# Pre-norms by one product with the mean on all partitions, a and b on four column groups, decode outputs transposed four heads at once

## The chip, the core and the metric

The kernel runs on one core of a Trainium2 chip. The metric is the device time of one execution in microseconds. The core has five engines that run side by side, each through its own instruction list in order: TensorE (PE in the profile; its weight loads are shown as PEld), VectorE (DVE), ScalarE (ACT), GpSimd (POOL) and SyncE (SP, which here only issues DMAs). They meet through semaphores. Activations and weights are in SBUF, matmul results in PSUM, which this kernel uses as eight banks of 128 partitions x 512 float32 values.

## The reference, cut to what matters

One layer of a hybrid decoder on 256 prompt tokens and 8 x 4 decode tokens, 288 columns in all, in float32. Every sub-layer has a norm before it and one behind it:

```python
def rmsnorm(x, g):
    y = x * lax.rsqrt(jnp.mean(x * x, axis=-1, keepdims=True) + EPS)
    return y * g

x = x + 0.5 * rmsnorm(swiglu(rmsnorm(x, f1_pre), f1_wg, f1_wu, f1_wd), f1_post)
proj = rmsnorm(x, mix_pre) @ w_in          # B, C, hc, q, k, v, z, a, b
...
g = -jnp.exp(a_log) * softplus(a + dt_bias)
beta = sigmoid(b)
o, s_new = gated_delta_chunked(l2norm(q) * 128**-0.5, l2norm(k), v, g, beta, s0)
o = rmsnorm(o, dn_norm) * silu(z)          # per head, transposed back in the kernel
out = concat([y_a, o], axis=-1) @ w_out
x = x + rmsnorm(out, mix_post)
x = x + 0.5 * rmsnorm(swiglu(rmsnorm(x, f2_pre), f2_wg, f2_wu, f2_wd), f2_post)
gate = sigmoid(rmsnorm(x, ple_pre) @ w_ple_gate)
x = x + rmsnorm(gate * (p @ w_ple_proj), ple_post)
```

The model width D is 2048, the FFN width 5632; a and b are 8 columns each of the mixer's input projection, one per head.

## The kernel before

**Layout.** Activations are kept transposed: features on the 128 partitions, the 288 tokens as columns. X holds 16 k-tiles of 128 x 288. The weights pass once from HBM as chunks of 128 x 512, four weight tiles of 128 x 128, on SP's DMA queue into six raw buffers. ACT casts a chunk to a rounded form `hi` (L133), DVE makes the remainder `lo` = raw - hi (L134); there are four buffers for such pairs. The activations are split in the same way into XH and XL. Each weight tile then costs three products of 288 columns: hi by XH (L361), hi by XL (L362) and lo by XH (L364). PE therefore spends nearly all its time on triples of these.

**Banks.** Five PSUM banks, "acc", form a ring for outputs that add up; three, "small", take everything else, and also the outputs beyond the fifth when more are open at a time.

**A matmul stage** (`gemm_steps`) starts with a group of outputs that advance together by k, since X itself is still being finished by the stage before: seven outputs in the FFNs and the gate, six in the mixer, five in the output projection. After that come outputs one by one. `prep(k)` finishes the k-tile k of X (adds the residual, squares it into the running sum `sq`, splits it) and is called four chunks ahead of the products that need it.

**The pre-norm** does not touch X. The products use unnormalised X with the gain folded in, and the norm's factor, one value per token, is multiplied into each output when it leaves PSUM: by L445 (`gu_t`) in the FFNs, L560 and L563 (`cvin`) in the mixer, L1132 (`gt`) in the gate. So it is needed when the first output of the first group is finished. `Later.after` makes it in three steps, one per chunk, once all k-tiles are through:

1. `join`: the two halves of the running sum are added (DVE).
2. `columns`: three products (L285) with a column of ones bring the sums of 128 tokens each onto the partitions, 128 x 3; the root (ACT), then on DVE v, a reciprocal, and a Newton step on 128 x 3 (L291, L229 to L232).
3. `kept`, with `rows`: three products (L300, L304) with the identity spread the factors over all partitions, and DVE copies the 128 x 288 result from PSUM (L310).

The mixer's value is `mix.value`, the gate's `ple.value`.

**a and b.** Their weights, 16 k-tiles of 128 x 16, lie in WS, split into 16 columns hi and 16 columns lo. `ab_side` (L587) runs behind each triple of the first output of the mixer's first group: two products, with XH and with XL, into a bank `ab` of 32 partitions, 32 products in all (L592). Their norm is L594, the gates' transposes are in `gates` (L631).

**Decode outputs.** Behind the delta rule, each head's output is transposed back (L960, L961 for the two prompt halves, L963 for the 32 decode tokens of that head, on 32 x 32) and multiplied with gain and z on DVE.

**Order.** The kernel is recorded in program order, and a scheduler sets the order of each engine's instructions when the program is built. An edit at one place can therefore move instructions of other places. In the mixer, `delta` is a generator that issues the gates and the delta rule step by step between the chunks of the input projection.

The functions that the change touches:

Of the kernel before, what the change touches and what calls it, by code (L numbers as in the profile page):

```python
# [41 lines left out]
GATE_START = 16  # L42
ROW_WAIT = 6
LAG = 1
SOLVE_STEPS = 2
# [100 lines left out]
def tile_hymba_step(ctx: ExitStack, tc: tile.TileContext, a: dict):  # L146
# [87 lines left out]
    epst = pers.tile([P, 1], F32, name="epst")  # L234
    nc.gpsimd.memset(epst, EPS)

    def sqrt_table(after):
# [6 lines left out]
    nc.gpsimd.memset(HOT, 0.0)  # L244
    nc.gpsimd.memset(HOT[:, 2:3], 1.0)

    class SquareSum:
# [29 lines left out]
        def columns(self, name, n_warm=0):  # L277
# [15 lines left out]
            rsqrt(self.cols, v, 3, s)  # L293

        def rows(self, name):

            pr = small(f"row_{name}")
            cols = self.cols
            for g in range(2):
                nc.tensor.matmul(  # L300
                    pr[:, g * P : (g + 1) * P], cols[:, g : g + 1].to_broadcast([P, P]), ID, start=True, stop=True
                )
# [24 lines left out]

    def gemm_steps(order, kt, rhs, done, prep=None, extra=None, rate=0, side=None, every=1, fill=(), fine=False):


# [3 lines left out]
        for c in range(len(order) // CH):  # L334
# [19 lines left out]
            for i in range(CH):  # L354
# [9 lines left out]
                nc.tensor.matmul(o, lo[:, i, :], xh, start=False, stop=seen[m] == kt)  # L364
                if side and m == order[0][0]:
                    side(k)
                if seen[m] == kt:
# [6 lines left out]
    def x_parts(k):  # L374
        return XH[:, k, :], XL[:, k, :]
# [38 lines left out]
    class Later:  # L414
# [91 lines left out]

    WS = tmp.tile([P, KD, 32], F32R, tag="qksq", bufs=1, name="WS")

    emb = []

    def loads():
# [19 lines left out]
        for _ in range(4):  # L531
            yield
        split(WS[:, :, 0:16], WS[:, :, 16:32], WR)

# [49 lines left out]

    finished, ab = [], []

    def ab_side(k):  # L587

        if k == 0:
            ab.append(small("ab")[:32, :N])  # L590
        for i, x in enumerate(x_parts(k)):
            nc.tensor.matmul(ab[0], WS[:, k, :], x, start=k == i == 0, stop=k == KD - 1 and i == 1)  # L592
# [38 lines left out]
    def gates():  # L631

        pab = small("pab")
        abd = dl.tile([P, 4, DT], F32, tag="junk", bufs=2, name="abd")
        nc.vector.tensor_copy(abd[:32], ABT[:32, None, SEQ:N].to_broadcast([32, 4, DT]))
        for g in range(3):
            src = ABT[:32, g * P : (g + 1) * P] if g < 2 else abd[:32].rearrange("p a b -> p (a b)")
            nc.tensor.matmul(pab[:, 16 * g : 16 * g + 16], src, C[:32, C_ID2 : C_ID2 + 16], start=True, stop=True)
        AB = tmp.tile([P, 3, 16], F32, tag="AB", bufs=1, name="AB")
# [267 lines left out]
    def delta():  # L907
        while 56 not in finished:
            yield
        for _ in range(GATE_START):  # L910
            yield
# [42 lines left out]
        YB = big.tile([P, H, N], F32, tag="LQ", name="YB")  # L954
        last.append(YB)
        for h in range(H):
            while 48 + h not in finished:
                yield
            po = small("oT")
            nc.tensor.transpose(po[:, 0:P], OB[:, h, :], ID)  # L960
            nc.tensor.transpose(po[:, P : 2 * P], OB[:, 8 + h, :], ID)  # L961
            r = slice(32 * (h % 4), 32 * (h % 4) + 32)
            nc.tensor.transpose(po[:, SEQ:N], OB[r, 16 + h // 4, :], ID[r, r])  # L963
            for c, z in ((slice(0, SEQ), V[:, h, :]), (slice(SEQ, N), VD[:, h, :])):
                nc.vector.scalar_tensor_tensor(
                    YB[:, h, c], po[:, c], C[:, C_DNN : C_DNN + 1], z, op0=ALU.mult, op1=ALU.mult
                )
            yield
# [46 lines left out]

    gemm(ORD["qkv"], KD, x_parts, qkv_done, mix, work, 1, ab_side, fill=fill_mix())
    mrow = mix.value
# [234 lines left out]
```

## Time and profile before

| | |
|---|---|
| Median of 3 runs | 2382.6 us (2380.88 to 2384.11) |
| Profiled execution, its own time | 2383.07 us |
| Span of that execution | 2381.3 us |
| Granted TensorE clock, mean | 0.997 |
| PE busy | 2357.7 us, 99% |
| DVE busy | 1473.1 us, 62% |
| ACT busy | 1165.9 us, 49% |
| POOL busy | 147.4 us, 6% |
| Read from HBM | 386.68 MB, 166 GB/s over the span |

How to read the profile's rows. A group row has the line, engine, operation, output <- input, the shape, and behind "x" the count; then the busy time in us and the mean of one in ns; then the idle time of the engine just ahead of these instructions, and what ended it. A timeline row begins with the start in us from the span's start and the time to the end of the row's last record; "x3" says that three records of one kind stand in it. A matmul's record is longer than the step from one to the next, since matmuls are pipelined: the pace is read from starts. A row of the list of waits has the waiting engine and tile, the releaser, and us in all, count and longest. A row of a windows table has the stretch and its length, then busy time and count of PE, PEld, DVE, ACT and POOL, the granted clock, the DMA share and the rate in GB/s. Numbers of a timeline come from the one profiled execution.

### The profile page before, as it was taken

How to read it: one execution, taken by the hardware profiler on the slowest of the kernel's cores; microseconds unless marked ns; L12 is line 12 of the kernel's file. 1: busy time of each engine (PE TensorE's matmuls, PEld its weight loads, DVE VectorE, ACT ScalarE, POOL GpSimd, SP SyncE). 2: the span in 40 equal slices, each digit the busy share in tenths (PEclk: the TensorE clock that was granted, in tenths of full speed). 3: DMA queues.
4: the chain of work that ended last, by engine and by line, in shares of the span. 5: the costliest groups of instructions: out<-in, count | busy, mean ns of one | idle time of the engine just before them, and what ended most of it. 6: DMA issues, size and time to landing. Idle time of an engine off the chain costs nothing.

```text
span 2381.3 us, 47494 instructions
## 1 busy us (share of the span) xinstructions
PE 2357.7 (99%) x17904; PEld 2336.5 (98%) x17904; DVE 1473.1 (62%) x2788; ACT 1165.9 (49%) x2222; POOL 147.4 (6%) x283
## 2 busy tenths in 40 slices
PE   9999999999999999999999999999999999999997
PEld 9999999999999999999999999999999999999997
DVE  6554555555555688888556577655555555555695
ACT  6444443444444567544455455544443444444474
POOL 0000000000000003122110002430000000000001
PEclk9999999999999999999999999999999999999999
DMA  7665665566656555565444566775656666666654
GB/s 233 172 165 166 167 166 167 165 168 165 167 166 167 166 161 147 162 188 162 129 140 129 167 174 175 226 216 165 168 165 166 167 167 165 166 167 166 187 156 124
DMA packets 213238, 399.07 MB, mean 168 GB/s; under 512 B 24183, under 2 KB 25616, under 8 KB 213008
## 3 DMA queue, kind: packets, MB, share of 16 engines
q1 hardware_dynamic: 207792, 377.73, 56.3%
q0 software_dynamic: 5072, 18.24, 2.5%
q8 instruction: 140, 2.29, 0.4%
q14 instruction: 90, 0.74, 0.1%
q10 hardware_dynamic: 144, 0.07, 0.0%
HBM read 386.68 MB, written 9.26 MB: 166 GB/s over the span
## 4 chain that ended last, share of the span: by engine, by line
PE 60%; DVE 1%; issue 0%; DMA 0%; ACT 0%; POOL 0%; DVEq 0%; ACTq 0%
PE acc L361 19%; PE acc L364 19%; PE acc L362 19%; DVE lo L134 0%; PE pkq L714 0%; DVE Y L1145 0%; PE po L882 0%; PE p L797 0%; DMA S<-in_state_delta 0%; PE pu L993 0%; PE pn L877 0%; DVE cvout L572 0%; PE p L787 0%; PE pd L893 0%; PE pS L870 0%
## 5 line engine op out<-in xcount | busy, mean ns | idle before, releaser
L134 DVE TENSOR_TENSOR lo<-raw,hi 128x512 fp32r<-128x512 f32 (+1 forms) x1417 | 990.5, 700 | 759.6 <-ACT hi L133 736.8
L133 ACT CAST hi<-raw 128x512 fp32r<-128x512 f32 (+1 forms) x1417 | 876.7, 620 | 1124.2 <-PE acc L362 1009.3
L361 PE MATMUL acc<-XH,hi 128*128 128x288 f32 x4096 | 1217.1, 298 | 2.2 <-ACT hi L133 1.2
L364 PE MATMUL acc<-XH,lo 128*128 128x288 f32 x4096 | 1213.1, 297 | 2.2 <-DVE lo L134 2.0
L362 PE MATMUL acc<-XL,hi 128*128 128x288 f32 x4096 | 1197.0, 292 | 0.0
L362 PEld LDWEIGHTS acc<-XL,hi 128*128 128x128 f32 x4096 | 780.4, 191 | 0.3 <-issue 0.2
L361 PEld LDWEIGHTS acc<-XH,hi 128*128 128x128 f32 x4096 | 770.4, 188 | 9.5 <-ACT hi L133 3.9
L364 PEld LDWEIGHTS acc<-XH,lo 128*128 128x128 f32 x4096 | 768.3, 188 | 3.7 <-DVE lo L134 3.3
L362 PE MATMUL acc<-hl_f,hi 128*128 128x288 f32 x1408 | 415.5, 295 | 0.0
L364 PE MATMUL acc<-hh_f,lo 128*128 128x288 f32 x1408 | 415.3, 295 | 0.0
L361 PE MATMUL acc<-hh_f,hi 128*128 128x288 f32 x1408 | 414.5, 294 | 0.0
L364 PEld LDWEIGHTS acc<-hh_f,lo 128*128 128x128 f32 x1408 | 264.8, 188 | 0.0
L362 PEld LDWEIGHTS acc<-hl_f,hi 128*128 128x128 f32 x1408 | 264.3, 188 | 0.0
L361 PEld LDWEIGHTS acc<-hh_f,hi 128*128 128x128 f32 x1408 | 264.0, 187 | 0.0
L445 DVE TENSOR_TENSOR gu_t<-acc,rows_ffn_f 128x288 f32<-128x288 f32 x176 | 79.9, 457 | 51.9 <-PE acc L364 51.6
L465 DVE TENSOR_TENSOR Y<-Y,acc 128x288 f32<-128x288 f32 x96 | 43.5, 453 | 28.1 <-PE acc L364 28.1
L558 POOL MEMSET cvin<- 128x3 f32 (+1 forms) x32 | 3.3, 102 | 900.9 <-PE acc L364 854.4
L1109 POOL DMA_DIRECT2D PJ<-pj_dram x3 | 1.6, 531 | 665.9 <-PE acc L364 665.9
L451 DVE TENSOR_TENSOR gu_t<-gu_t 128x288 f32<-128x288 f32 x88 | 41.3, 471 | 1.8 <-ACT gu_t L447 1.8
L319 ACT ACTIVATE XH<-X,G 128x288 fp32r<-128x288 f32 x64 | 34.3, 536 | 13.2 <-DVE X L398 12.9
L317 DVE TENSOR_TENSOR hl_f<-gu_t,hh_f 128x288 fp32r<-128x288 f32 x88 | 39.6, 452 | 0.0
L572 DVE SCALAR_TENSOR_TENSOR cvout<-cvin,CW,cvout 128x312 f32<-128x312 f32 x72 | 37.4, 536 | 2.9 <-ACT cvout L570 2.3
(369 smaller groups left out, 1239.3 us busy)
## 6 DMA issues: line engine op xcount, KB each, us to landing
raw<-in_gu SPq DMA_DIRECT2D x703, 256.0 KB, 2.7
raw<-in_dn SPq DMA_DIRECT2D x352, 256.0 KB, 2.7
raw<-in_qkv SPq DMA_DIRECT2D x96, 256.0 KB, 2.7
raw<-in_conv SPq DMA_DIRECT2D x96, 256.0 KB, 2.7
raw<-in_out SPq DMA_DIRECT2D x64, 256.0 KB, 2.7
raw<-in_gate SPq DMA_DIRECT2D x64, 256.0 KB, 2.7
raw<-in_z SPq DMA_DIRECT2D x32, 256.0 KB, 2.6
S<-in_state_delta POOLq DMA_DIRECT2D x8, 512.0 KB, 5.5
```

Source lines behind the costliest of these rows:

```text
L133: self.hi = nc.scalar.copy(hi[:, r], t[:, r]).ins
L134: nc.vector.tensor_tensor(lo[:, r], t[:, r], hi[:, r].bitcast(F32), op=ALU.subtract)
L317: nc.vector.tensor_tensor(lo, src, hi.bitcast(F32), op=ALU.subtract)
L319: first = nc.scalar.activation(hi, src, AF.Copy, scale=gain).ins
L361: nc.tensor.matmul(o, hi[:, i, :], xh, start=seen[m] == 0, stop=False)
L362: nc.tensor.matmul(o, hi[:, i, :], xl, start=False, stop=False)
L364: nc.tensor.matmul(o, lo[:, i, :], xh, start=False, stop=seen[m] == kt)
L445: nc.vector.tensor_tensor(t, ps, prep.value, op=ALU.mult)
L451: nc.vector.tensor_tensor(t, t, s, op=ALU.mult)
L465: nc.vector.tensor_tensor(Y[:, m, :], Y[:, m, :], ps, op=ALU.add)
L558: nc.gpsimd.memset(e[:, 0:w], 0.0)
L572: nc.vector.scalar_tensor_tensor(c[:, 0:n], e[:, j : j + n], wcols[:, j : j + 1], c[:, 0:n], op0=ALU.mult, op1=ALU.add)
```

## The change

**Pre-norms.** `SquareSum.direct` takes the place of `columns` and `kept` for the four pre-norms (both FFNs, mixer, gate); the norms behind the sub-layers stay as they were. One float32 product has the constant 0.25/D as its weights in all 128 x 128 places and the running squares as its 288 columns: every partition of the bank receives a quarter of the mean, for all tokens. ACT takes the root of it plus EPS/4 (s). DVE then makes r = 1/s, w = (ms + EPS/4) r + s, and 1/w on 128 x 288, which is the factor with one Newton step in it. `Later.after` has two steps in place of three.

**a and b.** WS holds the float32 weights, gain folded in, padded with zeros from 16 to 32 columns. `ab_products` issues 16 products with unsplit X together, on four groups of 32 PE columns by k modulo 4, so the bank holds four partial sums on 128 partitions. `delta` calls it AB_WAIT = 2 steps after the mixer's norm value has been made. The norm's multiplication (ABT) is on 128 partitions, and the gates' transposes add the four partial sums by contracting over 128 partitions.

**Decode outputs.** The 32 x 32 transpose per head goes; at every fourth head one 128 x 128 transpose brings the decode tokens of four heads, and one DVE operation multiplies them.

```diff
@@ SquareSum
+        def direct(self, name):
+            ps = small(f"ms_{name}")[:, :N]
+            for i, x in enumerate(self.parts):
+                nc.tensor.matmul(ps, MEAN.to_broadcast([P, P]), x, start=i == 0, stop=i == len(self.parts) - 1)
+            s = tmp.tile([P, N], F32, tag="rows", name=f"rs_{name}")
+            nc.scalar.activation(s, ps, AF.Sqrt, bias=epsq)
+            r, w = (tmp.tile([P, N], F32, tag=t, name=n) for t, n in (("e0", "rs_w"), ("e1", "rs_u")))
+            nc.vector.reciprocal(r, s)
+            nc.vector.scalar_tensor_tensor(w, ps, EPS / 4, r, op0=ALU.add, op1=ALU.mult)
+            nc.vector.tensor_tensor(w, w, s, op=ALU.add)
+            nc.vector.reciprocal(s, w)
+            return s
-        def kept(self, name):
-            pr = self.rows(name)
-            rows = tmp.tile([P, N], F32, tag="rows", name=f"rows_{name}")
-            nc.vector.tensor_copy(rows, pr)
-            return rows
@@ Later.after
             elif self.stage == 2:
-                self.sq.columns(self.name)
-            elif self.stage == 3:
-                self.value = self.sq.kept(self.name)
+                self.value = self.sq.direct(self.name)
@@ weights of a and b
-    WS = tmp.tile([P, KD, 32], F32R, tag="qksq", bufs=1, name="WS")
+    WS = tmp.tile([P, KD, 32], F32, tag="qksq", bufs=1, name="WS")
...
-        split(WS[:, :, 0:16], WS[:, :, 16:32], WR)
+        nc.vector.memset(WS[:, :, 16:32], 0.0)
+        gain = G[:, GAINS.index("mix_pre"), :, None].to_broadcast([P, KD, 16])
+        nc.vector.tensor_tensor(WS[:, :, 0:16], WR, gain, op=ALU.mult)
@@ mixer
-    def ab_side(k):
-        if k == 0:
-            ab.append(small("ab")[:32, :N])
-        for i, x in enumerate(x_parts(k)):
-            nc.tensor.matmul(ab[0], WS[:, k, :], x, start=k == i == 0, stop=k == KD - 1 and i == 1)
-        if k == KD - 1:
-            nc.vector.tensor_tensor(ABT[:32], ab[0], mix.value[:32], op=ALU.mult)
-            finished.append(56)
+    def ab_products():
+        ab = small("ab")[:, :N]
+        for k in range(KD):
+            r = slice(32 * (k % 4), 32 * (k % 4) + 32)
+            nc.tensor.matmul(
+                ab[r], WS[:, k, :], X[:, k, :], start=k < 4, stop=k >= KD - 4, tile_position=(0, 32 * (k % 4))
+            )
+        nc.vector.tensor_tensor(ABT, ab, mix.value, op=ALU.mult)
+        finished.append(56)
...
     def delta():
-        while 56 not in finished:
+        while mix.value is None:
+            yield
+        for _ in range(AB_WAIT):
             yield
+        ab_products()
@@ transposes of the outputs
-            nc.tensor.transpose(po[:, 0:P], OB[:, h, :], ID)
-            nc.tensor.transpose(po[:, P : 2 * P], OB[:, 8 + h, :], ID)
-            r = slice(32 * (h % 4), 32 * (h % 4) + 32)
-            nc.tensor.transpose(po[:, SEQ:N], OB[r, 16 + h // 4, :], ID[r, r])
...
+            for n in range(2):
+                nc.tensor.transpose(po[:, n * P : (n + 1) * P], OB[:, 8 * n + h, :], ID)
+            if h % 4 == 3:
+                nc.tensor.transpose(po[:, SEQ : SEQ + P], OB[:, 16 + h // 4, :], ID)
+                hs = slice(h - 3, h + 1)
+                gated(YB[:, hs, SEQ:N], po[:, SEQ : SEQ + P].rearrange("p (h t) -> p h t", h=4), VD[:, hs, :])
+            gated(YB[:, h, 0:SEQ], po[:, 0:SEQ], V[:, h, :])
```

What the scheduler makes of it, at three places. The numbers behind tile names count buffers, and the lines of the changed kernel are shifted: L134 is L135 there, L361, L362 and L364 are L374, L375 and L377, L560 and L563 are L572 and L575, L1132 is L1151.

DVE at the gate's pre-norm, before: the 128 x 3 operations, the copy, and the first outputs of the group (`gt`).

```order
L134 TENSOR_TENSOR lo_29064<-raw_28930,hi_29063 128x512
L291 TENSOR_SCALAR rs_v<-ss_ple 128x3
L229 RECIPROCAL rs_r<-rs_s 128x3
L230 SCALAR_TENSOR_TENSOR rs_t<-rs_r 128x3
L231 TENSOR_TENSOR rs_t<-rs_t,rs_v 128x3
L232 SCALAR_TENSOR_TENSOR rc_ple<-rs_t,rs_r 128x3
L134 TENSOR_TENSOR lo_29088<-raw_28948,hi_29087 128x512
L310 COPY rows_ple<-row_ple 128x288
L1132 TENSOR_TENSOR gt<-acc_28510,rows_ple 128x288
```

The same place in the changed kernel:

```order
L135 TENSOR_TENSOR lo_29002<-raw_28873,hi_29001 128x512
L309 RECIPROCAL rs_w<-rs_ple 128x288
L135 TENSOR_TENSOR lo_29020<-raw_28891,hi_29019 128x512
L310 SCALAR_TENSOR_TENSOR rs_u<-ms_ple,rs_w 128x288
L311 TENSOR_TENSOR rs_u<-rs_u,rs_ple 128x288
L135 TENSOR_TENSOR lo_29060<-raw_28914,hi_29059 128x512
L312 RECIPROCAL rs_ple<-rs_u 128x288
L135 TENSOR_TENSOR lo_29110<-raw_28932,hi_29109 128x512
L1151 TENSOR_TENSOR gt<-acc_28453,rs_ple 128x288
```

Where five narrow operations and the copy stood with one split between them, four wide operations now stand with two splits between them and a third ahead of the first `gt`.

PE at the mixer's norm, before: the three column sums stand between two triples, and two products for a and b behind each triple of the first output.

```order
L364 MATMUL acc_10549<-XH,lo_10917 128x288
L285 MATMUL ss_mix<-HOT,sq_pre_f_10433 128x3 x3
L361 MATMUL acc_10512<-XH,hi_10939 128x288
L362 MATMUL acc_10512<-XL,hi_10939 128x288
L364 MATMUL acc_10512<-XH,lo_10940 128x288
L592 MATMUL ab<-XH,WS 32x288
L592 MATMUL ab<-XL,WS 32x288
L361 MATMUL acc_10519<-XH,hi_10939 128x288
```

The same in the changed kernel:

```order
L374 MATMUL acc_10535<-XH,hi_10952 128x288
L304 MATMUL ms_mix<-sq_pre_f_10426,MEAN 128x288
L604 MATMUL ab<-X,WS 32x288 x16
L375 MATMUL acc_10535<-XL,hi_10952 128x288
L377 MATMUL acc_10535<-XH,lo_10953 128x288
L374 MATMUL acc_10539<-XH,hi_10952 128x288
L375 MATMUL acc_10539<-XL,hi_10952 128x288
L377 MATMUL acc_10539<-XH,lo_10953 128x288
L374 MATMUL acc_11142<-XH,hi_10980 128x288
```

The norm's product and all 16 products for a and b now stand together inside the triples of the last k-tile of the six-output group; `acc_11142`, five weight products behind, is the seventh output, the first one behind the group.

DVE at the mixer's norm in the changed kernel:

```order
L309 RECIPROCAL rs_w<-rs_mix 128x288
L310 SCALAR_TENSOR_TENSOR rs_u<-ms_mix,rs_w 128x288
L311 TENSOR_TENSOR rs_u<-rs_u,rs_mix 128x288
L135 TENSOR_TENSOR lo_11137<-raw_10911,hi_11136 128x512
L312 RECIPROCAL rs_mix<-rs_u 128x288
L572 TENSOR_TENSOR cvin<-acc_10505,rs_mix 128x256
L575 TENSOR_TENSOR cvin<-acc_10505,rs_mix 128x8x4
```

One split stands between the wide operations here, ahead of the second reciprocal; the first output of the group is read by the two `cvin` rows behind it.

More of the change, by code (lines that the diff above doesn't have):

```diff
@@ L43 @@
 ROW_WAIT = 6
+AB_WAIT = 2
 LAG = 1
@@ L235, in tile_hymba_step @@
     nc.gpsimd.memset(epst, EPS)
+    epsq = pers.tile([P, 1], F32, name="epsq")
+    nc.gpsimd.memset(epsq, EPS / 4)
     def sqrt_table(after):
@@ L245, in tile_hymba_step @@
     nc.gpsimd.memset(HOT[:, 2:3], 1.0)
+    MEAN = pers.tile([P, 1], F32, name="MEAN")
+    nc.gpsimd.memset(MEAN, 0.25 / D)
     class SquareSum:
@@ L326, in gemm, with gemm_steps @@
             pass
-    def gemm_steps(order, kt, rhs, done, prep=None, extra=None, rate=0, side=None, every=1, fill=(), fine=False):
+    def gemm_steps(order, kt, rhs, done, prep=None, extra=None, rate=0, every=1, fill=(), fine=False):
         acc, seen, ready = {}, {}, 0
@@ L364, in gemm_steps @@
                 nc.tensor.matmul(o, lo[:, i, :], xh, start=False, stop=seen[m] == kt)
-                if side and m == order[0][0]:
-                    side(k)
                 if seen[m] == kt:
@@ L955, in delta @@
         last.append(YB)
+        gated = lambda y, o, z: nc.vector.scalar_tensor_tensor(
+            y, o, C[:, C_DNN : C_DNN + 1], z, op0=ALU.mult, op1=ALU.mult
+        )
         for h in range(H):
@@ L1014, in fill_mix @@
         keep(0, PJ0)
-    gemm(ORD["qkv"], KD, x_parts, qkv_done, mix, work, 1, ab_side, fill=fill_mix())
+    gemm(ORD["qkv"], KD, x_parts, qkv_done, mix, work, 1, fill=fill_mix())
     mrow = mix.value
```

12 lines of the change are left out of this document (4 added, 8 removed).

## The prediction

> **What bounds the kernel now.** I read the page first, then the list of TensorE's waits, then the timeline around each place that the change touches.
>
> ```profile
> span 2381.3 us, 47494 instructions
> ...
> PE 2357.7 (99%) x17904; PEld 2336.5 (98%) x17904; DVE 1473.1 (62%) x2788; ACT 1165.9 (49%) x2222; POOL 147.4 (6%) x283
> ...
> L133 ACT CAST hi<-raw 128x512 fp32r<-128x512 f32 (+1 forms) x1417 | 876.7, 620 | 1124.2 <-PE acc L362 1009.3
> ```
>
> ```profile
> PE acc L364 <- DVE lo L134: 2.0, 2, 1.7
> ...
> PE ss_last L285 <- DVE sqt L1124: 0.2, 1, 0.2
> ```
>
> TensorE (PE) is busy 99% of the span, and its whole list of waits has ten rows, of 2.0 us down to 0.2 us; no pre-norm is among them. So PE time that goes away shortens the kernel, and any new PE wait lengthens it. ScalarE's (ACT's) casts sit idle 1009 us for PE: a weight chunk can be split only when PE has freed the buffer of the chunk four before it. What VectorE (DVE) does beside PE is free only as long as PE needs no result of it soon.
>
> **PE time that goes.** The pre-norm of the second FFN, with the products around it:
>
> ```profile
> 1445.81 0.30 PE L364 MATMUL acc<-XH,lo 128*128 128x288 f32 x1
> ...
> 1445.95 0.73 PE L285 MATMUL ss_ffn_f<-HOT,sq_pre_mix 128*128 128x3 f32 x6
> ...
> 1446.75 0.29 PE L362 MATMUL acc<-XL,hi 128*128 128x288 f32 x1
> ...
> 1448.46 0.29 PE L364 MATMUL acc<-XH,lo 128*128 128x288 f32 x1
> ...
> 1448.59 0.61 PE L300 MATMUL row_ffn_f<-C,rc_ffn_f 128*128 128x128 f32 x4
> ...
> 1449.70 0.30 PE L362 MATMUL acc<-XL,hi 128*128 128x288 f32 x1
> ...
> 1450.17 1.26 DVE L445 TENSOR_TENSOR gu_t<-acc,rows_ffn_f 128x288 f32<-128x288 f32 x3
> ```
>
> Weight products follow each other every 0.133 us (1445.81 to 1445.95), so two take 0.27. The first stretch holds 0.94 us, hence 0.67 for the three column sums; the second 1.24, hence 0.97 for the three row products: 1.64 us a norm. In their place stands one float32 product of 288 columns. The nearest row is the float32 product of 256:
>
> ```profile
> 989.71 0.30 PE L364 MATMUL acc<-XH,lo 128*128 128x288 f32 x1
> 989.84 0.59 PE L714 MATMUL pkq<-kq 128*128 128x256 f32 x2
> ...
> 990.52 0.29 PE L362 MATMUL acc<-XL,hi 128*128 128x288 f32 x1
> ```
>
> 0.81 less 0.27 is 0.54, with a 128-column transpose in it (about 0.05); 288/256 of the other 0.49, plus little, gives 0.57 us. Bounds: 0.49 and 0.65. Four pre-norms save 4 x 1.07 = **4.3 us**.
>
> For a and b, 32 products leave and 16 float32 products on four column groups come:
>
> ```profile
> 894.18 0.29 PE L592 MATMUL ab<-XH,WS 128*32 128x288 f32 x1
> ...
> 894.44 0.30 PE L361 MATMUL acc<-XH,hi 128*128 128x288 f32 x1
> ```
>
> ```profile
> 1051.61 0.29 PE L364 MATMUL acc<-XH,lo 128*128 128x288 f32 x1
> 1051.84 0.43 PE L861 MATMUL pSk<-S,EX 128*32 128x128 f32 x8
> 1052.08 0.40 PE L861 MATMUL pSq<-S,EX 128*32 128x128 f32 x8
> ...
> 1053.96 0.29 PE L362 MATMUL acc<-XL,hi 128*128 128x288 f32 x1
> ```
>
> Two old ones take 0.26, so 32 take 4.25. The state products of L861 have the new form: each row of 8 records is four float32 products of 128 columns on four groups, and the next begins 0.22 to 0.24 us later, where one such product alone needs half of the 256-column one, 0.21. So four run as one. All eight rows cost 2.35 - 0.27 = 2.08, of which 8 x 0.217 is pace and 0.34 entry and exit. Sixteen products of 288 are four such rows: 4 x 0.217 x 288/128 + 0.34 = 2.3 us, **1.95 saved**. One after the other they would cost 16 x 0.48 + 0.34 = 8.0, which loses 3.8: the other end.
>
> ```profile
> 1292.10 0.27 PE L960 MATMUL oT<-C,Y 128*128 128x128 f32 x1
> 1292.21 0.29 PE L961 MATMUL oT<-C,Y 128*128 128x128 f32 x1
> 1292.43 0.24 PE L963 MATMUL oT<-C,Y 32*128 32x32 f32 x1
> 1292.61 0.33 PE L960 MATMUL oT<-C,Y 128*128 128x128 f32 x1
> ```
>
> A head's three transposes take 0.51; two 128-wide ones take 0.22, and two more come in all: 8 x 0.51 - 18 x 0.11 = 2.1. Since six now stand together over three small banks that DVE must empty, I take **1.5**, between 0 and 2.1. The weights of a and b are made in the first FFN, where DVE and ACT have room: nothing. PE gains 7.75 in all.
>
> **What the new norm costs.** Five operations on 128x3 and a copy leave DVE; four on 128x288 come, two of them RECIPROCAL. No wide one was run; the narrow ones are these, with an ordinary operation for comparison:
>
> ```profile
> L229 DVE RECIPROCAL rs_r<-rs_s 128x36 f32<-128x36 f32 x1 | 0.4, 380 | 0.0
> ...
> L229 DVE RECIPROCAL rs_r<-rs_s 128x18 f32<-128x18 f32 x1 | 0.3, 267 | 0.8 <-ACT rs_s L226 0.8
> ...
> L231 DVE TENSOR_TENSOR rs_t<-rs_t,SKQ 128x36 f32<-128x36 f32 x1 | 0.2, 190 | 0.0
> ```
>
> At 36 columns it takes twice what its neighbour takes. From 18 to 36 columns it grows 113 ns, 6.28 ns a column, so 288 columns take 380 + 252 x 6.28 = **1.96 us**. The lower bound is an ordinary 288-column operation (0.46), the upper one the whole 380 ns as a price per column, 3.04. I take 1.96, since two points of the same operation give the slope. The Trainium skill ("VectorE: DVE Perf Modes", section "First, the fixed hardware budget") says that a reciprocal is an iterated division with a repeat count of 8; with the clock on the same page, 0.96 GHz, that would be an estimate of 2.4 us. The rows agree that it is dear and give six, not eight, cycles of that clock.
>
> The other prices:
>
> ```profile
> 47.36 0.72 PE L285 MATMUL ss_ffn_f<-HOT,sq_x 128*128 128x3 f32 x6
> ...
> 48.17 1.28 ACT L289 ACT_TABLE_LOAD   x1
> ```
>
> ```profile
> L445 DVE TENSOR_TENSOR gu_t<-acc,rows_ffn_f 128x288 f32<-128x288 f32 x176 | 79.9, 457 | 51.9 <-PE acc L364 51.6
> ...
> L397 DVE SCALAR_TENSOR_TENSOR res<-Y,gh_f,rows_post_f 128x288 f32<-128x288 f32 x28 | 14.1, 510 | 0.7 <-ACT rows_post_f L408 0.7
> ...
> L265 ACT ACTIVATE sqt<-Y 128x288 f32<-128x288 f32 x58 | 25.6, 442 | 4.9 <-DVE Y L465 3.3 <-DVE Y L1134 0.7
> ```
>
> Let T be the start of the new product. Its result is there at T+0.7 (the old sums show 0.73), the root at T+1.15. By the order of the changed program the gate norm then runs on DVE: RECIPROCAL to 3.1, a split (0.6) to 3.7, the two middle steps (0.51, 0.45) to 4.65, a split to 5.25, RECIPROCAL to 7.2, a split to 7.8, the first consumer to 8.2. Who waits: seven outputs of the first group are open, five in the "acc" banks, two in small ones. The eighth takes the first's bank and must wait until the consumer has read it. PE is there after the product (0.57) and three chunks of 12 weight products (3 x 1.59): T+5.35. **Stall 2.9 us**. In the profile of before the consumer is done by about T+4.6 (1450.17 plus a third of 1.26), and nothing waits. The second FFN's norm has the same order: 2.9 (two state products that now stand there fill at most some tenths). The first FFN's root stands behind the table load, which ends at 49.45: T+2.55. RECIPROCAL to 4.5, three splits and the two middle steps to 7.2, RECIPROCAL to 9.15, consumer to 9.6: **4.2**.
>
> In the mixer's norm the product moves to the end of the six-output group, and the a and b block stands right behind it, then five weight products: PE asks for the first bank at T + 0.57 + 2.3 + 0.67 = T+3.55. DVE: root 1.15, RECIPROCAL 3.1, middle steps 4.05; then a split whose cast waits for a buffer that PE frees four products behind the block, at T+3.4, cast 0.62: the split runs 4.05 to 4.65, RECIPROCAL to 6.6, the first consumer's two parts (about 0.6) to 7.2. **Stall 3.6**.
>
> The group ahead of it has one more price. There DVE prepares two k-tiles and six splits per round:
>
> ```profile
> 881.47 0.75 DVE L269 TENSOR_TENSOR sq_pre_f<-sq_pre_f,sqt 128x576 f32<-128x576 f32 x1
> 882.14 0.68 DVE L134 TENSOR_TENSOR lo<-raw,hi 128x512 fp32r<-128x512 f32 x1
> 882.74 0.45 DVE L398 TENSOR_TENSOR X<-X,res 128x288 f32<-128x288 f32 x1
> ...
> 886.40 0.75 DVE L269 TENSOR_TENSOR sq_pre_f<-sq_pre_f,sqt 128x576 f32<-128x576 f32 x1
> ```
>
> ```profile
> 869.00:877.00 8.00, 8.00 (x63) 7.87 (x62) 8.00 (x17) 5.47 (x10) 0.00 (x0) 1.00 0.52 136
> ```
>
> DVE is full (8.00 of 8.00) with 4.93 us a round. PE's round was 36 x 0.133 and four a/b products, 5.32; without these it is 4.79, shorter than DVE's. Eight rounds come out 8 x 0.14 = **1.1 us** late; prefetched splits could hide it all (0), and I take 1.1.
>
> **The sum.** 2.9 + 2.9 + 4.2 + 3.6 + 1.1 = 14.7 us of new waits, less 7.75: +6.95. The profiled execution took 2383.07 us, 0.5 over the median of the runs, so I count from the median: 2382.6 + 7.0 = **2389.6 us**. With the page's 2.4 us for each of the eight reciprocals the sum would be about 3.5 us higher, 2393.
>
> **Rivals.**
>
> First, the faster side: the eighth product finds a free bank, and PE works through its 6.4 us while DVE finishes the norm. Then the four stalls fall away: 2382.6 - 7.75 + 1.1 = 2376. For it: no pre-norm makes PE wait today. Against: five open outputs, ring of five; in the mixer six outputs, the norm and a/b hold all eight banks. It decides if the consumer is done before T+5.35. Chance 0.09.
>
> Second, RECIPROCAL is as cheap as its neighbours at this width (0.46). The chain is then paced by the splits: the one ahead of the consumer needs a buffer that PE frees at T+5.35, cast 0.62, split 0.6, consumer 0.45, so T+7.05 and a stall of 1.7 in the second FFN and the gate; 2.2 in the first FFN, 2.1 in the mixer: 7.7 + 1.1 - 7.75 = +1, 2383.7. For it only that nothing wide was measured. Chance 0.16.
>
> Third, the column groups of a/b run one behind the other: 8.0 in place of 2.3, 2395.3. L861's rows speak against it. Chance 0.06.
>
> Fourth, the wide RECIPROCAL is dearer than the line through 18 and 36 columns, midway to its upper bound at 2.5 us: eight times 0.54 on the chains, 2393.9. Chance 0.12. The skill's repeat count of 8 is this case; no wide row here shows it.
>
> **How the numbers follow.** My case holds 0.57, its own range 2386 to 2393.5. What this measurement can tell from no change is 0.2%, 4.8 us: 2377.8 and 2387.4. Some 0.07 of my case lie under 2387.4. Slower: 0.50 + 0.06 + 0.12 = 0.68; same: 0.16 + 0.07 = 0.23; faster: 0.09. The range reaches from under the second rival to over the third: 2381.5 to 2396.
>
> **What would show it.** RECIPROCAL 128x288 rows near 1.96 us, eight of them; four new PE waits of 3 to 4 us, for the DVE consumer of the first group; the norm's product at 0.57; a and b as four rows of eight records in 2.3 us; PE's busy time down while the span grows. A reciprocal near 0.5, or no PE wait behind the first groups, would make the prediction wrong.

## The result: 23 us slower, three times the forecast

The changed kernel takes 2405.93 us (median; 2404.75 to 2407.86), the kernel before 2382.65: ratio 1.0097, 95% interval 1.0085 to 1.0110. The direction was forecast, the size was not: +23.3 us where +7.0 stood, and 2405.9 lies outside the range, which ended at 2396. The profiled execution took 2406.8 us.

The page of the changed kernel, its span and its busy times:

```profile
span 2404.7 us, 47385 instructions
...
PE 2369.1 (99%) x17858; PEld 2346.0 (98%) x17858; DVE 1485.7 (62%) x2775; ACT 1167.0 (49%) x2221; POOL 145.6 (6%) x285
```

PE has 46 fewer records than before and is yet busy 11.4 us longer. The prediction had PE's busy time go down while waits come up. The list of PE's waits, its longest rows:

```profile
PE acc L374 <- DVE gu_t L454: 4.0, 1, 4.0
PE acc L374 <- DVE cvin L575: 3.9, 1, 3.9
PE acc L374 <- DVE gt L1151: 2.8, 1, 2.8
...
PE pu L1012 <- ACT new L1014: 0.7, 1, 0.7
```

The first three are the forecast waits for the first consumer of a norm: 4.2 foreseen in the first FFN, 3.6 in the mixer, 2.9 in the gate. In the second FFN state products stand in the gap, so that only 0.7 us is listed as a wait. The groups of the wide reciprocals:

```profile
L309 DVE RECIPROCAL rs_w<-rs_ffn_f 128x288 f32<-128x288 f32 x2 | 3.9, 1951 | 1.1 <-ACT rs_ffn_f L307 1.1
L312 DVE RECIPROCAL rs_ffn_f<-rs_u 128x288 f32<-128x288 f32 x2 | 3.9, 1948 | 0.0
```

1.95 us each, where 1.96 was taken from the line through 18 and 36 columns. And PE at the second FFN's norm and at the mixer's:

```profile
1457.46 0.29 PE L377 MATMUL acc<-XH,lo 128*128 128x288 f32 x1
1457.59 0.65 PE L304 MATMUL ms_ffn_f<-sq_pre_mix,MEAN 128*128 128x288 f32 x2
1457.86 0.51 PE L374 MATMUL acc<-XH,hi 128*128 128x288 f32 x1
1458.20 0.30 PE L375 MATMUL acc<-XL,hi 128*128 128x288 f32 x1
...
903.85 2.15 PE L604 MATMUL ab<-X,WS 128*32 128x288 f32 x32
905.93 0.40 PE L375 MATMUL acc<-XL,hi 128*128 128x288 f32 x1
```

From 1457.59 to 1458.20 is 0.61; less one weight product (0.13) the norm's product costs 0.48 (forecast 0.57). The 16 float32 products for a and b take 2.08 us (forecast 2.3), where 16 times the norm's 0.48 would be 7.7: the four column groups run side by side.

So nearly every price of the sum was right, and some 16 us are not in the sum at all. Two places show them. First, behind the wait of the first FFN:

```profile
52.50 0.29 PE L377 MATMUL acc<-XH,lo 128*128 128x288 f32 x1
56.81 0.58 PE L374 MATMUL acc<-XH,hi 128*128 128x288 f32 x1 [4.02 <-DVE gu_t L454]
57.19 0.44 PE L375 MATMUL acc<-XL,hi 128*128 128x288 f32 x1
57.43 0.44 PE L377 MATMUL acc<-XH,lo 128*128 128x288 f32 x1
...
60.07 0.37 PE L375 MATMUL acc<-XL,hi 128*128 128x288 f32 x1
60.28 0.30 PE L377 MATMUL acc<-XH,lo 128*128 128x288 f32 x1
60.41 0.29 PE L374 MATMUL acc<-XH,hi 128*128 128x288 f32 x1
```

Once released, PE takes 0.24 us a product (57.19 to 57.43) for 3.4 us, and only then 0.13 again. The granted clock in the table of stretches is 0.60 for 56 to 60 us (the column behind POOL's):

```profile
52.00:56.00 4.00, 0.79 (x6) 0.56 (x5) 4.00 (x6) 1.90 (x2) 0.00 (x0) 1.00 0.51 154
56.00:60.00 4.00, 3.19 (x13) 3.22 (x14) 3.96 (x12) 2.29 (x6) 0.00 (x0) 0.60 0.12 45
60.00:64.00 4.00, 4.00 (x31) 4.00 (x30) 2.43 (x6) 2.44 (x5) 0.00 (x0) 0.97 0.28 66
```

Some 14 products at 0.24 in place of 0.133 are 1.5 us. The changed kernel's profile has such a stretch behind each of the four norms, also behind the second FFN's, where PE's listed wait is 0.7 us. The kernel before has one too, which the prediction's reading passed over; it stands in the mixer, behind a wait of 1.75 us for a split:

```profile
912.00:916.00 4.00, 2.92 (x13) 2.92 (x14) 4.00 (x9) 2.17 (x6) 3.51 (x6) 0.68 0.30 85
```

Second, far from every edit. The casts of weight chunks in the first FFN's first matmul, where outputs go one by one, before and now (count; shortest, median and longest ns; start of the first and of the last):

```profile
L133 ACT CAST hi<-raw x38: 620/620/622, 290.7 to 349.4; 128x512 fp32r<-128x512 f32 x38
```

```profile
L134 ACT CAST hi<-raw x38: 620/620/621, 290.3 to 349.5; 128x512 fp32r<-128x512 f32 x38
```

37 chunks took 58.7 us before and 59.2 now: 1.587 and 1.600 us a chunk of twelve products. The FFNs alone have 704 such chunks, 9 us, and mixer and gate have more; with all 1024 whose moving operand is XH or XL it is some 13 us. No edit touches these products. What did change is where the weights lie: `epsq` and `MEAN` are two tiles of their own in the long-lived pool, each of which takes 32 bytes a partition. They stand behind XH and XL and ahead of the weight buffers, so the raw, hi and lo buffers and all that follows (the FFNs' hidden activations hh and hl too) begin 64 bytes later, while XH and XL stay. In a partition, XH begins at byte 43296 and XL at 61728 in both kernels, the first hi buffer at 111296 before and 111360 now, hh at 127680 and 127744. A k-tile of X is 1152 bytes, nine times 128, and a weight tile 512, so the distance between moving operand and weights modulo 128 is the same for all products of a kind: 96 before and 32 now for those with XH and XL, 0 in both for the down projections.

### The profile page after: what moved, and what is told of

Its sections match the earlier page's. It is cut to its first block, busy times and chain, and to the rows that moved or that the text cites. A ratio compares the mean times of both kernels' runs of the same rounds, so it can differ in the third digit from the quotient of the medians.

```text
span 2404.7 us, 47385 instructions
## 1 busy us (share of the span) xinstructions
PE 2369.1 (99%) x17858; PEld 2346.0 (98%) x17858; DVE 1485.7 (62%) x2775; ACT 1167.0 (49%) x2221; POOL 145.6 (6%) x285
## 4 chain that ended last, share of the span: by engine, by line
PE 59%; DVE 2%; issue 0%; DMA 0%; ACT 0%; DVEq 0%; ACTq 0%
PE acc L374 19%; PE acc L377 19%; PE acc L375 19%; DVE lo L135 0%; PE pkq L727 0%; DVE cvout L584 0%; PE pu L1012 0%; DMA S<-in_state_delta 0%; DVE Y L1164 0%; PE po L895 0%; PE p L810 0%; PE pn L890 0%; PE p L800 0%; PE pd L906 0%; PE pS L883 0%
## 5 line engine op out<-in xcount | busy, mean ns | idle before, releaser
L135 DVE TENSOR_TENSOR lo<-raw,hi 128x512 fp32r<-128x512 f32 (+1 forms) x1417 | 989.1, 699 | 767.0 <-ACT hi L134 745.3
L134 ACT CAST hi<-raw 128x512 fp32r<-128x512 f32 (+1 forms) x1417 | 876.9, 620 | 1146.2 <-PE acc L375 1028.2
L374 PE MATMUL acc<-XH,hi 128*128 128x288 f32 x4096 | 1217.8, 298 | 12.8 <-DVE gu_t L454 4.0
L377 PE MATMUL acc<-XH,lo 128*128 128x288 f32 x4096 | 1213.2, 297 | 1.9 <-DVE lo L135 1.7
L375 PE MATMUL acc<-XL,hi 128*128 128x288 f32 x4096 | 1214.9, 297 | 0.0
L374 PEld LDWEIGHTS acc<-XH,hi 128*128 128x128 f32 x4096 | 777.2, 190 | 21.1 <-issue 12.1
L377 PEld LDWEIGHTS acc<-XH,lo 128*128 128x128 f32 x4096 | 770.4, 188 | 3.2 <-DVE lo L135 2.8
L375 PEld LDWEIGHTS acc<-XL,hi 128*128 128x128 f32 x4096 | 771.9, 188 | 1.3 <-issue 0.7
L375 PE MATMUL acc<-hl_f,hi 128*128 128x288 f32 x1408 | 415.5, 295 | 0.0
L377 PE MATMUL acc<-hh_f,lo 128*128 128x288 f32 x1408 | 415.3, 295 | 0.0
L374 PE MATMUL acc<-hh_f,hi 128*128 128x288 f32 x1408 | 414.4, 294 | 0.0
L377 PEld LDWEIGHTS acc<-hh_f,lo 128*128 128x128 f32 x1408 | 264.8, 188 | 0.0
L375 PEld LDWEIGHTS acc<-hl_f,hi 128*128 128x128 f32 x1408 | 264.4, 188 | 0.0
L374 PEld LDWEIGHTS acc<-hh_f,hi 128*128 128x128 f32 x1408 | 264.0, 188 | 0.0
L454 DVE TENSOR_TENSOR gu_t<-acc,rs_ffn_f 128x288 f32<-128x288 f32 x176 | 79.7, 457 | 53.9 <-PE acc L377 53.6
L456 ACT ACTIVATE gu_t<-gu_t 128x288 f32<-128x288 f32 x88 | 39.0, 445 | 2.7 <-DVE gu_t L454 2.6
```

The costliest lines, as they stand in the source:

```text
L134: self.hi = nc.scalar.copy(hi[:, r], t[:, r]).ins
L135: nc.vector.tensor_tensor(lo[:, r], t[:, r], hi[:, r].bitcast(F32), op=ALU.subtract)
L374: nc.tensor.matmul(o, hi[:, i, :], xh, start=seen[m] == 0, stop=False)
L375: nc.tensor.matmul(o, hi[:, i, :], xl, start=False, stop=False)
L454: nc.vector.tensor_tensor(t, ps, prep.value, op=ALU.mult)
L456: nc.scalar.activation(t, t, AF.Silu)
```

## The experiments

All ratios are to the kernel before, with 95% intervals.

### The place of the weights

Theory: the 64 bytes between moving operand and weights set the pace. Rival: the changed instructions or their order do. `fit` is the changed kernel with the two constants in unused columns of a tile that was there:

```diff
-    epsq = pers.tile([P, 1], F32, name="epsq")
-    MEAN = pers.tile([P, 1], F32, name="MEAN")
-    HOT = pers.tile([P, 5], F32, name="HOT")
+    HOT = pers.tile([P, 8], F32, name="HOT")
+    epsq, MEAN = HOT[:, 6:7], HOT[:, 7:8]
```

> The changed kernel with its two new constants put into the unused end of the tile HOT, so that the weight buffers stand where they stood before, 64 bytes nearer to XH and XL; instructions and order are the same. Layout theory (the weight products with XH and XL got slower because of those 64 bytes): about 11 us less than the changed kernel, 2394.5 us (2392.5 to 2396), triples of the FFNs' first matmul back from 400 to 397 ns; the four stalls behind the norms and the half-clock stretches stay. Rival (the slower pace comes from the changed instructions or their order): 2405 to 2407 us.

Measured 2394.46 us, ratio 1.0052 (1.0037 to 1.0068): 11.5 us of the 23.3 are gone, with the same work on every engine. `pad64` does the reverse, the kernel before with two unused constants:

```diff
+    PAD0 = pers.tile([P, 1], F32, name="PAD0")
+    nc.gpsimd.memset(PAD0, 0.25 / D)
+    PAD1 = pers.tile([P, 1], F32, name="PAD1")
+    nc.gpsimd.memset(PAD1, 0.25 / D)
```

> The kernel before with two unused constants as tiles of their own, at the place of the changed kernel's, so that only the weight buffers and all behind them move by 64 bytes. Layout theory: 2382.7 plus about 11, 2393.5 us (2391.5 to 2395), with the FFNs' triples at 400 ns and the down projections unchanged. Rival (order or instructions): 2382.7 us, within 2.

Measured 2395.9 us, ratio 1.0058 (1.0042 to 1.0074): 13.3 us for two four-byte constants that nothing reads, a little more than the range that was expected (up to 2395). The cast row for the same place:

```profile
L133 ACT CAST hi<-raw x38: 620/620/621, 290.1 to 349.3; 128x512 fp32r<-128x512 f32 x38
```

59.2 us, as in the changed kernel. Is it the distance, or where the weights lie by themselves? `xmove` leaves the weights and moves XH and XL by 64 bytes (with Y and a few small tiles behind them), by allocating a small tile earlier:

```diff
+    CAP = pers.tile([P, 8, 2], F32, name="CAP")
     XH = pers.tile([P, KD, N], F32R, name="XH")
...
-    CAP = pers.tile([P, 8, 2], F32, name="CAP")
```

> The kernel before with one small tile (64 bytes a partition) put ahead of XH in place of behind Y: XH and XL move by 64 bytes, the weight buffers and the hidden activations stay where they were. Distance theory (the distance between moving operand and weights decides; modulo 128 it goes from 96 to 32, as in the changed kernel): 1.600 us a chunk in the first FFN matmul, down projections 1.595 as before, 2394 to 2396 us. Rival (the place of the weight buffers by itself decides: modulo 128 they began at 64 in the kernel before and at 96 in shift_a, both fast, at 0 in pad64 and 32 in shift_b, both slow): 1.587 us, 2382.7 us.

Measured 2396.26 us, ratio 1.0053 (1.0038 to 1.0067), and its row:

```profile
L133 ACT CAST hi<-raw x38: 619/619/621, 289.7 to 348.9; 128x512 fp32r<-128x512 f32 x38
```

59.2 us again, with every weight where it was. So the place of the weights alone is not it, nor is that of XH and XL, which `pad64` left alone: the distance is. Two more distances, with one unused constant and a gap ahead of the hidden activations (`shift_a`), and with three and a larger gap (`shift_b`):

```diff
+    gap = ctx.enter_context(tc.tile_pool(name="gap", bufs=1))
     big = ctx.enter_context(tc.tile_pool(name="big", bufs=1))
...
+    GAP = gap.tile([P, 16], F32, name="GAP")
+    PAD0 = pers.tile([P, 1], F32, name="PAD0")
```

> The kernel before with the weight buffers 32 bytes further (one unused constant) and the FFNs' hidden activations another 64 bytes further, so that the distance between moving operand and weights modulo 128 bytes is 64 both for products with XH and XL (before 96, pad64 32) and for the down projections (before and pad64 0). Layout theory, distance modulo 128 alone decides: both kinds of FFN products run at one and the same pace, which no run has shown yet; a chunk of the first FFN matmul took 1.5867 us at distance 96 and 1.6000 at 32, one of the down projection 1.5951 at 0. Rival (the absolute place, or a larger modulus, decides): two different paces.

> The kernel before with the weight buffers 96 bytes further (three unused constants) and the hidden activations another 96 bytes further: distance 0 for the products with XH and XL, 96 for the down projections, the two distances of before exchanged. Layout theory: the first FFN matmul takes the old pace of the down projection (1.595 us a chunk), the down projection the old pace of the first (1.587); with twice as many chunks of the first kind and those of the mixer and the gate: about 6 us slower for these, 3 us faster for the down projections, 2386 us (2384 to 2388). Rival (distance modulo 128 is not what decides): one of the two paces does not follow.

`shift_a` 2378.92 us, ratio 0.9987 (0.9978 to 0.9996); `shift_b` 2389.8 us, 1.0030 (1.0018 to 1.0042). Their rows for the first matmul and then for a down projection, `shift_a`:

```profile
L133 ACT CAST hi<-raw x38: 621/623/623, 290.4 to 349.1; 128x512 fp32r<-128x512 f32 x38
L133 ACT CAST hi<-raw x32: 619/621/623, 395.1 to 444.4; 128x512 fp32r<-128x512 f32 x32
```

`shift_b`:

```profile
L133 ACT CAST hi<-raw x38: 621/622/624, 290.7 to 349.9; 128x512 fp32r<-128x512 f32 x38
L133 ACT CAST hi<-raw x32: 619/621/622, 394.5 to 443.8; 128x512 fp32r<-128x512 f32 x32
```

And the down projection of the kernel before:

```profile
L133 ACT CAST hi<-raw x32: 620/621/625, 395.5 to 445.0; 128x512 fp32r<-128x512 f32 x32
```

The starts in these rows are given to 0.1 us, so a pace read from them is good to 0.003 us. The table is sharper: twelve times the mean step between the starts of neighbouring products, over all products of a kind in the trace. By distance modulo 128 bytes, in us a chunk:

| distance | 96 | 64 | 32 | 0 |
|---|---|---|---|---|
| products with XH and XL | 1.587 (before) | 1.587 (shift_a) | 1.600 (changed), 1.601 (pad64, xmove) | 1.598 (shift_b) |
| down projections | 1.590 (shift_b) | 1.588 (shift_a) | not run | 1.595 (before) |

Both kinds are faster at 64 and 96 than at 0 (and 32), and in `shift_a`, where both have distance 64, they run at nearly one pace, as was expected. But `shift_b` did not simply exchange the two paces, as was expected of it: the products with XH take 1.598 at distance 0, the down projections 1.595, and 1.587 stands against 1.590 at 96; its time lies above the expected 2384 to 2388. So distance modulo 128 is not the whole rule; what else enters (the distance of hl from hh, or a larger modulus) was not tried.

### The half clock

Theory: the stretch of 0.24 us a product is the answer to PE's idle time ahead of it. `warmfill` is `fit` with unneeded products in that idle time, into free columns of the norm's own bank; `fill1` has those of the first FFN alone; `fit2` is `fit` again beside it.

```diff
+FILLER = {"ffn_f1": 38, "ple": 27}
...
                 self.value = self.sq.direct(self.name)
+            elif self.stage == 5 and self.name in FILLER:
+                for _ in range(FILLER[self.name]):
+                    nc.tensor.matmul(self.sq.bank[:, N:512], XH[:, 0, 0:P], XH[:, 1, 0 : 512 - N], start=True, stop=True)
```

> As fit, and in the idle time of PE behind the norm of the first FFN and of the gate stand 38 and 27 unneeded products of 224 columns, about 3.9 and 2.8 us of PE time, directly ahead of the product that waits; their results go to no output. Clock theory (the half-clock stretch of 3.4 us is the answer to the idle time): the stretches behind these two norms vanish, the one in the second FFN and the one in the mixer stay; each costs 14 products at 0.24 instead of 0.133 us, 1.5, so 3.0 us less than fit: 2391.5 us. Rival (the stretches come whatever PE does, or follow from something else): the time of fit, or up to 0.5 us more.

> As fit, with the 38 unneeded products ahead of the waiting product of the first FFN's norm alone (their results go to no output). Clock theory: the half-clock stretch behind that norm is gone, nothing else moves: 2 us less than the same fit on the same chip (in the profile of the kernel with both fillers that place gained 2.1). Rival: no difference (within 0.5).

> fit once more, beside the kernel with one filler. 2394.5 us; waits of 4.0, 3.9 and 2.8 us behind the norms of the first FFN, the mixer and the gate, each followed by a half-clock stretch of 3.4 us or more.

The same two stretches in `fit2`, where PE idled 4.0 us ahead of them:

```profile
56.00:60.00 4.00, 3.43 (x14) 3.46 (x15) 4.00 (x11) 2.54 (x6) 0.00 (x0) 0.50 0.06 24
60.00:64.00 4.00, 4.00 (x24) 4.00 (x23) 1.93 (x5) 1.57 (x4) 0.00 (x0) 0.68 0.24 66
```

and in `fill1`:

```profile
56.00:60.00 4.00, 4.00 (x35) 4.00 (x34) 3.97 (x12) 2.13 (x5) 0.00 (x0) 1.00 0.14 53
60.00:64.00 4.00, 4.00 (x33) 4.00 (x32) 3.36 (x8) 2.72 (x6) 0.00 (x0) 1.00 0.12 16
```

The granted clock is 0.50 and 0.68 without the filler and 1.00 with it, and behind this place the chunks of `fill1` run 2.0 us ahead of those of `fit2`. In `warmfill` both stretches are gone. That the half clock answers the idle time is shown. The totals say less: `fit2` 2394.02 us, 1.0046 (1.0032 to 1.0060); `fill1` 2392.97, 1.0042 (1.0030 to 1.0055), 1.05 us less with intervals that overlap; and `warmfill` 2394.94, 1.0057 (1.0039 to 1.0075), not the 3.0 less that was expected. In its gate the gain turned into another wait, 8.5 us behind the filler (ACT's rows, then PE's):

```profile
2320.23 0.53 ACT L1160 ACTIVATE Y<-Y,G 128x288 f32<-128x288 f32 x1
2320.68 0.60 ACT L135 CAST hi<-raw 128x512 fp32r<-128x512 f32 x1
```

```profile
2321.33 0.40 PE L376 MATMUL acc<-XH,hi 128*128 128x288 f32 x1 [1.95 <-ACT hi L135]
```

PE waits 1.95 us for a cast, and ACT has no idle time ahead of that cast: it stands in ACT's order behind the gate's own outputs. Why ACT is behind here and not in `fit` was not followed further.

The traces also show why one wait brings a stretch and another does not. Within one profile the half-clock stretches begin whole multiples of 3.413 us apart: in the changed kernel at 56.82, 910.15, 1466.52 and 2326.68 us, which is 250, 163 and 252 such steps. Laid on this grid, every step at full clock in which PE waited 1.8 us or more, about half of it, was followed by one at half clock; of those with 1.7 us or less none was, but for the one in the second FFN; 1.75 us was followed by one and 1.79 (`xmove`) was not. The wait of 1.75 us in the kernel before lies whole within one step (910.02 to 913.43), so it counts as much as a longer one that is divided between two. Why a wait of 4.0 us brings one stretch or two follows in the same way: in the changed kernel 3.4 us of it filled one step, in `fit` 2.5 us lay in one step and 1.5 in the next.

### The reciprocals

`one` writes the Newton step without the second wide RECIPROCAL, in the same places of DVE's order; `bare` has the root and one RECIPROCAL alone. Both stand on `fit`.

```diff
             nc.vector.reciprocal(r, s)
             nc.vector.scalar_tensor_tensor(w, ps, EPS / 4, r, op0=ALU.add, op1=ALU.mult)
-            nc.vector.tensor_tensor(w, w, s, op=ALU.add)
-            nc.vector.reciprocal(s, w)
+            nc.vector.scalar_tensor_tensor(w, w, -0.25, r, op0=ALU.mult, op1=ALU.mult)
+            nc.vector.scalar_tensor_tensor(s, w, 0.75, r, op0=ALU.add, op1=ALU.mult)
```

> As fit, but the Newton step is written without the second wide RECIPROCAL: (0.75 - w/4) r in place of 1/w, one operation of about 0.5 us in the same place of DVE's order. Reciprocal theory (the stall is the length of DVE's chain, of which each RECIPROCAL is 1.95): each chain 1.45 us shorter, so the waits go from 4.0 to 2.55 (first FFN), 3.9 to 2.45 (mixer), 2.8 to 1.35 (gate), and the second FFN gains up to 1.45; together 5 to 5.8 less than fit, 2389 us, and up to 4 less again if the shorter waits bring no half-clock stretch: 2385 to 2389.5. Rival (the splits that stand in DVE's chain, waiting for buffers, set its end): 2393 to 2395.

Measured 2385.28 us, 1.0011 (1.0002 to 1.0021): 9.2 less than `fit`. Its waits:

```profile
PE acc L373 <- DVE gu_t L453: 2.5, 1, 2.5
PE acc L373 <- DVE cvin L574: 2.4, 1, 2.4
...
PE acc L373 <- DVE gt L1150: 0.9, 1, 0.9
```

Against 4.0, 3.9 and 2.8, each RECIPROCAL taken off DVE's chain shortens PE's wait by its own excess over an ordinary operation, 1.5 us (1.9 in the gate, more than the excess; not followed further). These are 4.9 of the 9.2; the second FFN's shorter stall, which the list hides, and missing half-clock stretches are the rest, and were not told apart. In the profiled execution none of the listed waits is followed by such a stretch, and that is partly luck: on the grid of 3.41 us the 2.5 us fall into two steps with 0.9 and 1.6, the 2.4 us with 0.7 and 1.7. Other executions of `one` had a mean clock from 0.997 (2383.67 us) down to 0.995 (2387.96 us).

```diff
-            nc.scalar.activation(s, ps, AF.Sqrt, bias=epsq)
+            nc.scalar.activation(s, ps, AF.Sqrt, bias=epsq, scale=4.0)
...
+            nc.vector.reciprocal(s, s)
+            return s
```

> As fit, with ACT's root and one wide RECIPROCAL alone: the Newton step is left out. DVE's chain loses 1.95 and the two middle operations (0.9): first FFN done at T + 5 to 5.6 and gate at T + 4.5, with PE at the waiting product at T + 5.35; mixer done at T + 4.4 with PE at T + 3.55. Reciprocal theory: no wait in both FFNs and the gate (0.3 at most), 0.8 in the mixer, no half-clock stretch behind the FFNs and the gate: 2394.5 - 13 - 5 = 2376.5 us (2375 to 2379), below the kernel before. Rival (PE would wait for something else, a split or a bank): 2380 to 2388.

Measured 2377.18 us, 0.9975 (0.9965 to 0.9985). Of the four waits one is left:

```profile
PE acc L369 <- DVE cvin L570: 0.3, 1, 0.3
```

`bare` also gives the stall of the second FFN, which the list of waits hides. The norm's product and, behind the stall, the cast of one and the same chunk, in `bare`:

```profile
1440.68 0.65 PE L303 MATMUL ms_ffn_f<-sq_pre_mix,HOT 128*128 128x288 f32 x2
...
1523.07 0.65 ACT L134 CAST hi<-raw 128x512 fp32r<-128x512 f32 x1
```

and in `fit`:

```profile
1451.61 0.65 PE L303 MATMUL ms_ffn_f<-sq_pre_mix,HOT 128*128 128x288 f32 x2
...
1537.08 0.65 ACT L134 CAST hi<-raw 128x512 fp32r<-128x512 f32 x1
```

10.9 us apart at the norm and 14.0 behind it: 3.1 us, where 2.9 was forecast.

### a and b and the transposes without the new norm

`abt` has the change without its pre-norms: `Later.after` calls `columns` and `kept` as before.

```diff
             elif self.stage == 2:
-                self.value = self.sq.direct(self.name)
+                self.sq.columns(self.name)
+            elif self.stage == 3:
+                self.value = self.sq.kept(self.name)
```

> The kernel before with the change's a and b and its transposes, but the old pre-norm; weight buffers where they were. By the prediction's steps: 1.95 saved for a and b, 1.5 for the transposes, 1.1 lost in the DVE-bound group of the mixer: 2382.7 - 2.35 = 2380.3 us. By the trace of the changed kernel (4 us gained up to the mixer's norm, 2.1 for the a and b block, 2.1 for the transposes): 2378.7. No half-clock stretch beyond the one of before, and no PE wait behind the norms. Rival (the a and b block, now all behind the norm, makes a new wait in the mixer): 2383 to 2385.

Measured 2380.37 us, 0.9992 (0.9983 to 1.0002): 2.3 less than before, as the prediction's steps have it, though the interval just takes in no change. Its trace divides the gain in another way. Across the output transposes its chunks gain 2.2 us on those of the kernel before. The a and b block saves 2.2 us of PE time, but PE's waits in the mixer grow: 0.5 us that is new, for the norm's factor (`row_mix`), and 3.4 in place of 2.0 us for splits. By difference the new pre-norms cost 2394.46 - 2380.37 = 14.1 us.

### Both gains together

`best` is `bare` with the layout of `shift_a`.

> bare with the layout of shift_a (weight buffers 32 bytes further, hidden activations another 64): the two gains are in different places, so they add: 2377.2 less the 0.007 us of each of the 352 down-projection chunks (2.5) and some tenths in the output projection, 2374.3 us (2373 to 2376). Rival (the gains overlap or the layout's gain was the chance of a missing half-clock stretch): 2376.5 to 2378.

Measured 2372.8 us, 0.9963 (0.9949 to 0.9977): 10 us less than the kernel before and 33 less than the changed one, as two gains that add would have it, though the interval overlaps with that of `bare`. Like `bare`, it leaves out the Newton step.

## Why the prediction was wrong

**What bounds the kernel**: right. A PE wait lengthened the time by its full length, or by more where half clock followed, and a shorter one gave it back.

**PE time that goes**: right. 0.48 for 0.57 a norm, so 4.6 in all for 4.3. The a and b block saves 4.25 - 2.08 = 2.2 for 1.95, the transposes 2.2 for 1.5. That `abt` measures 2.3, just 1.95 + 1.5 - 1.1, is luck: these two parts give 4.4, and what takes most of the difference off again is new waits in the mixer (0.5 and 1.4 us) that the prediction does not have.

**RECIPROCAL**: right, 1.95 for 1.96; the second and the fourth rival fall, and with a and b at 2.08 us the third. The estimate of 2.4 us from the Trainium skill ("VectorE: DVE Perf Modes", section "First, the fixed hardware budget") falls too: from 36 to 288 columns the rows give 1.57 us for 252, 6.2 ns or six cycles of that page's 0.96 GHz a column, not eight.

**The stalls**: right in mechanism and size: 4.0, 3.9, 2.8 and 3.1 for 4.2, 3.6, 2.9 and 2.9, 13.8 for 13.6. The first rival, a free bank, falls.

**The 1.1 us of the mixer's first group**: at most half of it. PE ran 120 products in 16 us there, its own pace of 0.133:

```profile
865.00:881.00 16.00, 16.00 (x120) 15.80 (x119) 15.51 (x32) 11.98 (x24) 0.97 (x3) 1.00 0.64 203
```

DVE was busy 15.51 of 16 us, and just kept up; over the whole group the few longer steps between PE's products come to some 0.5 us.

**The sum**: here it failed, by two terms that it puts at nothing without a reason: what follows a PE wait, which it prices at its length alone, and where the two new constants push the weight buffers. With the measured prices of the terms that it has, it is 13.8 - 4.6 - 2.3 = +6.9, almost the forecast +6.95. `fit`, which has all of the change but the shift, is +11.8, inside the range. The other 4.9 are the half clock: in the profile of `fit` PE worked 13.2 us at half clock (5.3, 4.8 and 3.0 us in three places), in that of the kernel before 3.4, and half of the difference is 4.9. The shift of the weights is the last 11.5 (2405.93 - 2394.46; `pad64` alone gives 13.3). The intervals reach 2 to 4 us to either side, so that the sum closes to the tenth is chance.

The half clock could have been foreseen: the trace of the kernel before has 0.68 behind a wait of 1.75 us, and the prediction forecast four longer waits. The Trainium skill ("TensorE: Matmul & The Clock Gate", section "HAM oscillation — how this bites in real kernels") says to leave PE no idle gap over about 3.4 us. The traces here do not bear that limit out: the gate's 2.8 us brought a stretch in each of the profiles that has it (the changed kernel, `fit`, `fit2`, `fill1`), and so did the 1.75 us. Waits of 2.5 and 2.4 us in `one` brought none; where a wait falls on the grid of 3.41 us matters beside its length.

The shift could not be read from the profile of before; it could be read from the kernel's whole diff, as two tiles in a pool that is laid out ahead of the weights. "The weights of a and b ... nothing" was costed, the two constants were not. That the distance matters was not known from any row; the pace of 1.587 against 1.595 in the two FFN matmuls of the kernel before, with the same number of products a chunk, was the only sign.

## What to carry to other kernels

Where PE is the bound, price a new wait with what comes behind it: here each wait of 2.8 us or more cost another 1.5 us or more at half clock, unless PE was given other products meanwhile. Before adding even a four-byte constant, look at what is laid out behind it, and compare the pace of untouched loops in the first trace after a change: a difference of 0.8% there was half of the loss. A value that a matmul spreads over 128 partitions is cheap on PE and dear on DVE when a reciprocal must then run on all its columns: one of them could be hidden, two with a Newton step between them could not.

## What the runs showed of the hardware that was not expected

The same twelve products of a chunk take 1.587 or 1.600 us by the distance in SBUF between their moving operand and their weights: 96 and 64 bytes modulo 128 fast, 32 and 0 slow, by 0.8%; for the down projections 1.588 to 1.590 and 1.595. Over the kernel the two constants' shift is 11.5 to 13.3 us, more than the whole change was forecast to cost. PE's half-clock stretches of 3.4 us begin on a grid of 3.413 us, and follow a step of it in which PE waited about half of the time or more: a wait of 2.8 us brought one every time, waits of 1.75 (kernel before), 1.8 (`pad64`) and 2.1 us (`one`) that lay within one step brought one, and 2.5 us divided between two steps brought none. Behind the second FFN's norm one came with only 0.7 us of listed wait, while PE ran small state products; why is not shown. Filling the wait with unneeded products removes the stretch.
